# Seven products for eight: Strassen's form in a transformer layer's first MLP product

## The chip, the cores and the metric

The kernel runs on one core of one Trainium2 chip. The metric is the device time of one execution in microseconds; the figure for the kernel before is the median of three runs. Engines are called as in the profile: PE is TensorE's matmul, PEld its weight load, DVE VectorE, ACT ScalarE, POOL GpSimd, SP SyncE (here only a DMA queue).

## The reference

Two layers of a hybrid trunk over 512 latent tokens and 256 context tokens, width 1024, hidden width 4096. In each layer a modulated norm feeds one input projection, whose columns go to a gated mixer and to attention; an output projection and a gated residual follow, and then the part that matters here:

```python
x_lat = x_lat + ga2 * sqrelu_mlp(modulate(rmsnorm(x_lat, norm2_g[l]), sh2, sc2), w_ff1[l], w_ff2[l])
# the same for x_ctx in layer 0 only

def sqrelu_mlp(h, w1, w2):
    return jnp.square(jax.nn.relu(h @ w1)) @ w2
```

The shifts, scales and gates come from `silu(c) @ w_mod[l] + b_mod[l]`, six vectors of 1024 for the latents and, from `c_ctx`, for the context. In layer 1 no context output is wanted, so only its first shift and scale are needed.

## The kernel before

Activations lie feature-major: 128 features on the partitions, 768 tokens (512 latent, 256 context) along the free axis. Each float32 operand is held as two float32r tiles: `hi`, a rounded copy, and `lo`, the rest. A product of two operands is three matmuls, hi·hi, hi·lo and lo·hi, added up in PSUM. `split` makes the two parts: `act.copy` writes `hi` (L207), a subtraction on DVE writes `lo` (L208).

Weights come in blocks of 128 x 1024 float32 (512 KB) in the order that `block_order` writes down. `pump` issues the next load on SP's queue into one of two `raw` buffers and splits it into one of four `hi`/`lo` slots; `take` hands a block to a product, `release` gives its slot back, and after a delay in the program's virtual time (`fl`, a clock in ns that the matmuls advance) `settle` pumps again.

The MLP of a layer is `ff1_first` and then `steady`:

- `ff1_first` computes the first four hidden tiles (128 hidden features each, 8 k-tiles deep) while the norm's two parts, context and latents, get ready one after the other.
- A chunk `ch` of `steady` is four hidden tiles. It runs one `ff1` tile of the next chunk, the second product's share of this chunk (`proj4`: 8 output tiles of 4 k-tiles, `gate` L790 adds each from PSUM into the residual `X`, scaled), and three more `ff1` tiles. Layer 0's tokens go in two parts of 384 (`DENSE`), so a hidden tile is 8 x 3 x 2 = 48 matmuls.
- `relu2` turns a hidden tile in PSUM into squared relu, again as `hi` and `lo`: ACT relu (L960), ACT square (L965), DVE square and subtraction (L966, L967).

Beside layer 0's MLP run layer 1's modulation vectors (`mod_wide`): for each of 12 columns of 512, eight loads of 256 KB; per load and condition ACT multiplies by the input (L374), POOL adds (L375); then DVE transposes and reduces (L386, L387) and four tiny matmuls finish (L392). `more()` emits the next step of that generator. `consts` prepares a layer's constants (rotary factors `G`, norm gains, the mixer's weights): two loads on ACT's queue, one on SP's, small DVE operations (L566 to L579).

The order in which each engine issues is made by a list scheduler when the program is built. Inside `manual_schedule(engines=...)` the named engines keep the order in which the code emits; the others are reordered. For layer 0's MLP, `PAR["FM0"]` is `'DA'`: DVE and ACT keep the emitted order in chunks 0 to 6.

## Time and profile before

| what | value |
|---|---|
| median of three runs | 1515.79 us (1515.77 to 1517.52) |
| the profiled execution: its time | 1516.59 us |
| its span, first to last instruction | 1514.8 us |
| granted TensorE clock, mean | 0.995 |
| instructions | 22788, of these 8804 matmuls |
| DMA | 148.83 MB, mean 98 GB/s |

Layer 0's MLP lies at about 380 to 915 us of the span, layer 1's begins near 1200. How to read the lines that follow: in the page's part 2 each digit is the busy share, in tenths, of one fortieth of the span (37.9 us). A row of a group is line, engine, operation, `out<-in`, shape, count, then busy us, mean ns of one instruction, and the engine's idle time just before these with the one that ended it. Matmuls are pipelined, so the mean of one is longer than the distance between two; rates are taken from a count in a stretch of time.

### The profile page before, as it was taken

Reading aid. Unit: us, or ns where it says so; the run is one execution under the profiler, and the core shown is the slowest. Engines: PE = TensorE matmul, PEld = TensorE weight load, DVE = VectorE, ACT = ScalarE, POOL = GpSimd, SP = SyncE. Lnnn points to the kernel's source line nnn. Section 1 sums busy time; section 2 is a strip of 40 time slices with the busy share of each in tenths; the row PEclk is TensorE's granted clock in tenths of the full one; section 3 lists DMA queues with packets and bytes.
Section 4 is the critical chain, followed back from the end, with each engine's and each line's share of the span. In section 5 each row is a group of like instructions: output and inputs, shape, how many; then the busy total and the mean of one; then the engine's idle time right before and its main releaser. Section 6 shows DMA issues by size and latency. Waiting matters only on the chain.

```text
span 1514.8 us, 22788 instructions
## 1 busy us (share of the span) xinstructions
PE 1463.9 (97%) x8804; PEld 1316.3 (87%) x8804; DVE 959.7 (63%) x1874; ACT 682.4 (45%) x1142; POOL 403.5 (27%) x362
## 2 busy tenths in 40 slices
PE   6999899999999999999999999998999999999998
PEld 2899687787899999999999988996899888888887
DVE  5877967787755455555555548888887644444443
ACT  3542455674445454544545334535784333322221
POOL 0112421312054555554545513044212000000000
PEclk9999999999999999999999999999999999999999
DMA  9221344401234333343434311321001323333332
GB/s 362 66 71 55 118 177 156 138 1 42 74 105 132 112 112 125 112 125 98 134 103 127 107 45 56 98 70 56 29 1 56 112 98 98 98 97 97 96 95 76
DMA packets 49948, 148.83 MB, mean 98 GB/s; under 512 B 5424, under 2 KB 6832, under 8 KB 49840
## 3 DMA queue, kind: packets, MB, share of 16 engines
q1 hardware_dynamic: 49264, 146.46, 30.2%
q8 instruction: 69, 1.13, 0.3%
q10 hardware_dynamic: 576, 0.92, 0.2%
q14 instruction: 39, 0.32, 0.1%
HBM read 145.26 MB, written 2.10 MB: 97 GB/s over the span
## 4 chain that ended last, share of the span: by engine, by line
PE 79%; DVE 12%; ACT 3%; DMA 3%; issue 1%; POOL 0%; SPq 0%; ACTq 0%; DVEq 0%; POOLq 0%
PE pa L203 51%; PE pb L203 20%; PE pt L203 3%; PE pt L850 3%; DVE lo L208 1%; PE pb L332 1%; ACT hi L207 1%; DMA raw<-in_w_tok 1%; DMA B<-in_w_mod 1%; DMA A<-in_w_mod 1%; DVE m L283 1%; DVE B L967 1%; DVE m L831 1%; ACT w L834 1%; DVE A L853 1%
## 5 line engine op out<-in xcount | busy, mean ns | idle before, releaser
L203 PE MATMUL pa<-A,hi 128*128 128x384 f32 (+2 forms) x1696 | 449.1, 347 | 1.9 <-ACT w L960 0.6
L207 ACT CAST hi<-raw 128x1024 fp32r<-128x1024 f32 x171 | 179.5, 1050 | 408.9 <-PE pa L203 325.9
L208 DVE TENSOR_TENSOR lo<-raw,hi 128x1024 fp32r<-128x1024 f32 x155 | 203.3, 1312 | 216.5 <-ACT hi L207 213.1
L203 PEld LDWEIGHTS pa<-A,hi 128*128 128x128 f32 x1696 | 304.7, 188 | 26.0 <-ACT w L960 1.8
L375 POOL TENSOR_TENSOR C<-C,s 128x512 f32<-128x512 f32 x168 | 240.4, 1462 | 244.7 <-ACT s L374 244.7
L203 PE MATMUL pa<-A,lo 128*128 128x384 f32 (+2 forms) x848 | 293.6, 347 | 1.1 <-DVE lo L208 1.1
L203 PE MATMUL pa<-B,hi 128*128 128x384 f32 (+1 forms) x900 | 246.5, 356 | 4.4 <-DVE X L790 4.4
L203 PEld LDWEIGHTS pa<-B,hi 128*128 128x128 f32 x900 | 162.9, 188 | 21.6 <-DVE X L790 9.4
L790 DVE SCALAR_TENSOR_TENSOR X<-pa,modT,X 128x384 f32<-128x384 f32 (+1 forms) x168 | 88.0, 547 | 141.9 <-PE pa L203 141.7
L203 PEld LDWEIGHTS pa<-A,lo 128*128 128x128 f32 x848 | 159.3, 188 | 12.3 <-DVE lo L208 1.5
L203 PE MATMUL pa<-B,lo 128*128 128x384 f32 (+1 forms) x450 | 158.1, 353 | 0.0
L203 PE MATMUL pb<-B,hi 128*128 128x256 f32 (+2 forms) x600 | 152.8, 341 | 0.4 <-DVE X L790 0.4
L374 ACT ACTIVATE s<-k,silu 128x512 f32<-128x512 f32 x168 | 114.3, 716 | 47.1 <-DMA k<-in_w_mod 27.6
L203 PE MATMUL pb<-hi,A 128*128 128x256 f32 x672 | 126.2, 285 | 0.0
L203 PEld LDWEIGHTS pb<-B,hi 128*128 128x128 f32 x600 | 103.9, 189 | 11.4 <-DVE X L790 1.0
L790 DVE SCALAR_TENSOR_TENSOR X<-pb,modT,X 128x512 f32<-128x512 f32 (+3 forms) x116 | 69.0, 602 | 69.0 <-PE pb L203 68.8
L203 PEld LDWEIGHTS pb<-hi,A 128*128 128x128 f32 x672 | 106.1, 191 | 0.2 <-issue 0.2
L203 PE MATMUL pb<-B,lo 128*128 128x256 f32 (+2 forms) x300 | 101.6, 339 | 0.0
L203 PE MATMUL pb<-lo,A 128*128 128x256 f32 x336 | 95.3, 284 | 0.0
L203 PEld LDWEIGHTS pa<-B,lo 128*128 128x128 f32 x450 | 84.4, 188 | 5.9
L434 POOL TENSOR_TENSOR acc<-acc,s 128x256 f32<-128x256 f32 (+1 forms) x43 | 47.0, 1092 | 138.7 <-ACT s L432 138.2
L834 ACT ACTIVATE w<-pa,m 128x768 f32<-128x768 f32 (+1 forms) x80 | 65.7, 821 | 38.2 <-DVE m L831 29.8
(171 smaller groups left out, 2321.9 us busy)
## 6 DMA issues: line engine op xcount, KB each, us to landing
raw<-in_w_ff SPq DMA_DIRECT2D x128, 512.0 KB, 3.5
k<-in_w_mod SPq DMA_DIRECT2D x96, 256.0 KB, 2.9
raw<-in_w_tok SPq DMA_DIRECT2D x19, 512.0 KB, 3.6
raw<-in_w_out SPq DMA_DIRECT2D x16, 512.0 KB, 3.5
lo<-in_w_mod SPq DMA_DIRECT2D x16, 512.0 KB, 4.5
hi<-in_w_mod SPq DMA_DIRECT2D x16, 512.0 KB, 3.7
A<-in_w_mod SPq DMA_DIRECT2D x8, 512.0 KB, 10.0
raw<-in_w_u SPq DMA_DIRECT2D x8, 512.0 KB, 3.6
```

The costliest lines, as they stand in the source:

```text
L203: pe.matmul(out, a, b, start=start, stop=stop)
L207: act.copy(hi, src)
L208: (eng or vec).tensor_tensor(out=lo, in0=src, in1=hi.bitcast(F32), op=ALU.subtract)
L283: vec.tensor_scalar(yi, v.bitcast(I32), -0.5, 1595932665.0, op0=ALU.mult, op1=ALU.add)
L332: pe.matmul(ps[q:q + 32, :], S32[:, k, :], ws_[k2 // 2][:, k2 % 2 * 512:(k2 % 2 + 1) * 512], start=k < ns, stop=k >= KT - ns)
L374: act.activation(p, w, AF.Copy, scale=s)
L375: pool_e.tensor_tensor(out=a, in0=a, in1=p, op=ALU.add)
L434: eng.tensor_tensor(out=self.acc, in0=self.acc, in1=sq, op=ALU.add)
L790: vec.scalar_tensor_tensor(out=xs, in0=src[:, s - off:e - off], scalar=modT[l][:, i * 8 + m, cond:cond + 1], in1=xs, op0=ALU.mult, op1=ALU ...
L831: vec.tensor_reduce(out=nmx, in_=ps[:, 0:nk], axis=AX.X, op=ALU.max, negate=True)
L834: act.activation(p, ps[:, 0:nk], AF.Exp, bias=nmx, accum_out=sm)
L850: pe.transpose(tp_[:, (kt - k0) * 128:(kt - k0) * 128 + 128], p[:, kt * 128:kt * 128 + 128], ident)
```

## The change

In layer 0 the first product is done, for 14 pairs of hidden tiles (p, p + 16), in the form of Strassen as Winograd wrote it: weights in a 2 x 2 grid (hidden halves by input halves), tokens in a 2 x 2 grid (input halves by token halves of 384), seven block products and additions before and after instead of eight products. The other four tiles (0, 16, 1, 17) stay in `ff1_first`.

- Weights: a new `factor` loads both tiles of a pair, splits a11 and a12 (`al`), forms four differences and sums on POOL in place, then splits the sums (`be`), the differences (`ga`) and a22 (`q`, in a pair of half-wide tiles of its own).
- Tokens: `factors` forms the token sums `TT` once, from the second pass of `ff1_first` through chunk 0's second product (POOL adds hi and lo, DVE subtracts, ACT and DVE split).
- `ff1_pair` runs the seven products on four PSUM banks, with ACT copies and DVE and POOL adds between, and squares the relus.
- Hidden tiles get buffers of their own, H0 to H3, one each; in a chunk both pairs come first, then the second product, whose first three output tiles run their first half of k ahead (`early`). Its parts are 512 and 256 instead of 384 and 384 in all of layer 0's chunks.
- `FM0` is `''`: all engines are reordered in layer 0's MLP.
- `mod_wide` leaves out the context half of eight columns, yields after nearly each add instead of each load, and defers its last step by `MF`; it starts in chunk 1, not 0.
- Layer 1's `consts` move from before the steady chunks to behind chunk 7. Several small tiles move into H0 to H3, and the scratch of dynamic DMAs is set to 1024 bytes. The rows of `w_ff2` are laid out in the new order of hidden tiles.

The diff, cut to its core:

```diff
-       "FM0": 'DA', "FM1": '', ...
+       "FM0": '', "FM1": '', ...  "MF": 6000.0, ...
@@ block_order
+        if l == 0:
+            o += [("ff1", l, m) for m in (0, 16, 1, 17)]
+            for ch in range(8):
+                if ch:
+                    a, b = 2 * ch, 2 * ch + 1
+                    o += [("al", l, a), ("be", l, a), ("al", l, b), ("ga", l, a), ("be", l, b), ("ga", l, b)]
+                o += [("ff2", l, ch, nb) for nb in range(4)]
+            continue
@@ beside pump
+    def factor(key):
+        kind, l, p = key
+        hi, lo = slot()
+        if kind == "al":
+            ra = ring.tile([128, 1024], F32, tag="raw", name=nm("raw"), bufs=2)
+            nc.sync.dma_start(ra, w_ff1[l, p])
+            rb = unit(("B6", "C0")[p % 2], [128, 1536], F32)
+            nc.sync.dma_start(rb[:, 512:1536], w_ff1[l, p + 16])
+            raws[p] = ra, rb
+            split(hi, lo, ra)
+            a11, a12, s2, a21, a22 = ra[:, 0:512], ra[:, 512:1024], rb[:, 0:512], rb[:, 512:1024], rb[:, 1024:1536]
+            tt = pool_e.tensor_tensor
+            tt(out=a11, in0=a11, in1=a21, op=ALU.subtract)
+            tt(out=a21, in0=a21, in1=a22, op=ALU.add)
+            tt(out=s2, in0=a22, in1=a11, op=ALU.subtract)
+            tt(out=a12, in0=a12, in1=s2, op=ALU.subtract)
+        elif kind == "be":
+            split(hi, lo, raws[p][1][:, 0:1024])
+        else:
+            ra, rb = raws.pop(p)
+            split(hi, lo, ra)
+            qh, ql = (ring.tile([128, 512], F32R, tag=t, name=nm(t), bufs=1) for t in ("qh", "ql"))
+            split(qh, ql, rb[:, 1024:1536])
+            ready.append((("q", l, p), qh, ql))
+        ...
@@ mod_wide
+            conds = range(2 if j < 4 else 1)
+            acc = unit("C1", [128, 3, 512], F32)
...
-                if k not in PAR["YK"]:
-                    yield
+                    if k > 1 or k and cond:
+                        yield
...
+            fl.defer(PAR["MF"], fin)
@@ consts
+        kg = unit("H2", [128, 1664], F32)
+        k2 = kg[:, 0:640]
...
+        ws = unit("H3", [128, 2, 512])
@@ proj4: the first three output tiles, first half of k ahead
+                    if early and pi == 0 and m < 3:
+                        if m == 0:
+                            ...
+                            for i in range(3):
+                                for q, (off, n) in enumerate(parts):
+                                    fm_mms(ed[i][q][:, 0:n], ew[i], off, n, 0, 2)
+                                fl.tick()
+                        for q, (off, n) in enumerate(parts):
+                            fm_mms(ed[m][q][:, 0:n], ew[m], off, n, 2, 4)
+                            gate(i_, m, off, n, ed[m][q])
+                            ...
@@ layer
+        def product(dst, w, wo, rhs, first, last_):
+            for k in range(4):
+                whi, wlo = (a[:, wo + k * 128:wo + k * 128 + 128] for a in w)
+                rhi, rlo = rhs(k)
+                for i, (a, b) in enumerate(((whi, rhi), (whi, rlo), (wlo, rhi))):
+                    pe.matmul(dst, a, b, start=first and k == 0 and i == 0, stop=last_ and k == 3 and i == 2, skip_group_check=True)
+                    fl.vt += hn / 2.4 + 13.0
+            fl.tick()
+
+        def ff1_pair(p):
+            ...
+            ps = pa()
+            A, C = ps[:, 0:hn], ps[:, 512:512 + hn]
+            B, E = pb()[:, 0:hn], pt()[:, 0:hn]
+            ...
+            al = take("al", l, p)
+            product(A, al, 0, quad(0, 0), True, True)
+            act.copy(c1_, A)
+            be = take("be", l, p)
+            product(C, be, 512, tsum(0), True, True)
+            act.copy(c5, C)
+            more()
+            product(A, al, 512, quad(1, 0), False, True)
+            release()
+            r = tsm([128, hn])
+            act.activation(r, A, AF.Relu)
+            hd = H[p]
+            act.activation(hd[:, 0, 0:hn], r, AF.Square)
+            tt(out=r, in0=r, in1=r, op=ALU.mult)
+            tt(out=hd[:, 1, 0:hn], in0=r, in1=hd[:, 0, 0:hn].bitcast(F32), op=ALU.subtract)
+            more()
+            product(B, be, 0, tsum(1), True, True)
+            release()
+            tt(out=U2, in0=B, in1=c1_, op=ALU.add)
+            more()
+            product(E, take("q", l, p), 0, tsum(3), True, True)
+            ga = take("ga", l, p)
+            product(B, ga, 0, tsum(2), False, True)
+            tt(out=U3, in0=B, in1=c1_, op=ALU.add)
+            pool_e.tensor_tensor(out=c5, in0=c5, in1=U3, op=ALU.add)
+            t21 = tsm([128, hn])
+            tt(out=t21, in0=E, in1=U3, op=ALU.add)
+            put(p + 16, 0, sqrelu(t21))
+            more()
+            product(C, ga, 512, quad(1, 1), False, True)
+            release()
+            tt(out=U2, in0=C, in1=U2, op=ALU.add)
+            put(p, 1, sqrelu(U2))
+            put(p + 16, 1, sqrelu(c5))
+            more()
@@ steady
+                if strassen:
+                    if ch:
+                        ff1_pair(2 * ch)
+                        ff1_pair(2 * ch + 1)
+                    R = [H.pop(m) for m in (2 * ch, 2 * ch + 16, 2 * ch + 1, 2 * ch + 17)]
...
-                passes, post = [list(dense)], None
+                passes, post = [[(0, SEQ), (SEQ, CTX)] if strassen else list(dense)], None
...
+                if strassen:
+                    if end:
+                        K1.append(consts(l + 1))
```

`put(m, j, sq)` writes token half j of a hidden tile: ACT copies `hi`, DVE subtracts `lo`. `sqrelu` is one DVE operation.

## The prediction

> **What bounds the kernel now.** First the page: which engine has no time left.

> ```profile
> span 1514.8 us, 22788 instructions
> PE 1463.9 (97%) x8804; PEld 1316.3 (87%) x8804; DVE 959.7 (63%) x1874; ACT 682.4 (45%) x1142; POOL 403.5 (27%) x362
> PE   6999899999999999999999999998999999999998
> DVE  5877967787755455555555548888887644444443
> POOL 0112421312054555554545513044212000000000
> PEclk9999999999999999999999999999999999999999
> PE 79%; DVE 12%; ACT 3%; DMA 3%; issue 1%; POOL 0%; SPq 0%; ACTq 0%; DVEq 0%; POOLq 0%
> ```

> TensorE (PE) is busy 97% of the span at full clock, and 79% of the chain that ended last is matmuls. A busy PE need not be an efficient one, so the next view cuts layer 0's MLP, which the change rewrites, at its chunk boundaries (columns: stretch, its us, then busy us and instructions of PE, weight load, VectorE (DVE), ScalarE (ACT), GpSimd (POOL), clock, DMA share, GB/s).

> ```profile
> 383.00:408.00 25.00, 24.34 (x113) 19.72 (x113) 20.60 (x31) 13.04 (x22) 3.51 (x2) 1.00 0.17 53
> 408.00:554.20 146.20, 145.27 (x847) 142.55 (x846) 81.43 (x111) 72.21 (x97) 74.10 (x52) 1.00 0.39 120
> 623.00:692.00 69.00, 68.16 (x402) 66.81 (x402) 35.99 (x50) 32.93 (x45) 33.34 (x25) 1.00 0.36 111
> 833.90:895.00 61.10, 61.10 (x352) 58.16 (x351) 31.51 (x49) 22.32 (x29) 19.33 (x14) 1.00 0.31 92
> ```

> One steady chunk (four hidden tiles of the first product, then a quarter-depth part of the second) takes 69.0 us; DVE is busy 52% of it, ACT and POOL 48%. Next, the rate inside a chunk, from pieces of the chain of waits (start, us, what, count), and all of PE's waits from 383 to 895 us (total, times, longest):

> ```profile
> 572.75 2.08 PE pa L203 x12
> 939.32 5.46 PE pb L203 x24
> 982.38 5.81 PE pb L203 x48
> ```

> ```profile
> PE pa L203 <- DVE X L790: 4.4, 5, 1.3
> PE pa L203 <- ACT w L960: 0.6, 1, 0.6
> ```

> Twelve 384-wide matmuls take 2.08 us: 173.3 ns each. The other pieces, from layer 1, are 512 wide (227.5 ns) and 256 wide (121.0 ns). A steady chunk has 4 x 48 + 192 = 384 matmuls of 384, which is 66.6 us; 2.4 us of 69.0 are small modulation matmuls and stalls, and PE's own waits come to only 5.0 us in 512. This stage is matmuls end to end: what is taken from PE comes off the time, until another engine cannot keep up.

> **The change part by part.** *Matmuls.* For two hidden tiles p and p+16 the old form issues 2 x 8 x 3 x 2 = 96 matmuls of 384, the new one 7 products x 4 x 3 = 84. Tiles 0, 16, 1, 17 keep the old form, so 14 pairs change: 168 x 173.3 ns = **-29.1 us**. The second product's 512+256 costs 348.5 ns where 384+384 costs 346.7: 7 chunks x 96 x 1.8 ns = **+1.2 us** (chunk 7 has these parts already). A chunk is then 29.1 + 33.5 = 62.6 us of matmuls.

> *What pays for it: DVE, ACT, POOL.* The rows from 410 to 890 us (busy us, mean ns, idle before), and POOL's adds over the run (min/median/max ns):

> ```profile
> L208 DVE TENSOR_TENSOR lo<-raw,hi 128x1024 fp32r<-128x1024 f32 x57 | 82.8, 1453 | 107.7 <-ACT hi L207 107.7
> L967 DVE TENSOR_TENSOR B<-w,B 128x768 fp32r<-128x768 f32 x24 | 36.6, 1527 | 0.8
> L966 DVE TENSOR_TENSOR w<-w 128x768 f32<-128x768 f32 x27 | 25.8, 957 | 9.9 <-ACT B L965 8.9 <-ACT C L965 0.7
> L790 DVE SCALAR_TENSOR_TENSOR X<-pa,modT,X 128x384 f32<-128x384 f32 x42 | 25.7, 613 | 13.1 <-PE pa L203 12.9
> L386 DVE STREAM_TRANSPOSE s<-C 128x512 f32<-128x512 f32 x24 | 16.8, 702 | 0.0
> L387 DVE TENSOR_REDUCE m<-s 128x16 f32<-128x512 f32 x24 | 16.5, 686 | 0.8
> L569 DVE TENSOR_TENSOR G<-w,k 128x128 f32<-128x128 f32 x4 | 1.1, 282 | 0.0
> L208 DVE TENSOR_TENSOR ws<-raw,ws 128x512 fp32r<-128x512 f32 x1 | 0.7, 693 | 0.8 <-ACT ws L207 0.8
> ```

> ```profile
> L374 ACT ACTIVATE s<-k,silu 128x512 f32<-128x512 f32 x166 | 112.9, 716 | 45.7 <-DMA k<-in_w_mod 27.6 <-POOL C L375 17.9
> L207 ACT CAST hi<-raw 128x1024 fp32r<-128x1024 f32 x57 | 59.8, 1048 | 149.9 <-PE pa L203 135.7 <-PE pt L203 14.2
> L960 ACT ACTIVATE w<-pa 128x512 f32<-128x512 f32 x2 | 1.2, 590 | 0.0
> ```

> ```profile
> L375 POOL TENSOR_TENSOR C<-C,s x168: 1274/1296/2292, 393.9 to 860.6; 128x512 f32<-128x512 f32 x168
> ```

> DVE, per pair: weight splits 3 x 1.45 + 0.69 = 5.0 us (before 2.9); four adds out of PSUM x 0.61 = 2.4 and eight 384-wide SBUF operations, half a 768-wide row each (0.48 to 0.76, taken as 0.7), 5.6, against 2 x (0.96 + 1.53) = 5.0 before. That is +5.1 us a pair, 71 us in 14. The gates lose their third instruction, and eight modulation columns lose their context half (8 x 1.39 = 11 us). A chunk has about 43 us of DVE, 69% of 62.6. ACT: casts 3 x 1.05 + 0.62 and seven 384-wide operations of about 0.5 per pair, four casts for the second product (4.2 us) and some 17 modulation multiplies x 0.716 per chunk (18 steps of one each, less those that transpose): 31 us, 49%. POOL: four weight sums x 1.46 and one 384-wide add near 1.1 per pair, 17 modulation adds x 1.46: 39 us, 62%. None is full, so I price this work at nothing beside PE and pay for the places where its latency can show:

> - *Inside a pair* two matmul groups accumulate on a bank that another engine must read first: product 3 behind ACT's copy of A, product 6 behind DVE's first U2 add. The cover of each is one product, 2.08 us. The add takes 0.61, so it may come 1.4 us late; a DVE instruction that has just started takes up to 1.5, rarely more. Bounds per pair: nothing, to 1.0 us (blocked splits at both places). I take 0.3, nearer the low end, as most of DVE's instructions are far shorter than 1.4: **+4.2 us**.
> - *Chunk ends.* No next tile stands between the pairs and the second product now; its first three output tiles run on the first pair's hidden tiles instead, 3 x 6 x 348.5 ns = 6.3 us of cover. The last tiles need the U2 add, two squared relus, two copies and two low parts: 4 to 5 us of DVE, 6 to 7.5 with a split in between. Before, a chunk paid up to 2.4 us here. Bounds for the difference: -2 to +3 a chunk; I take **0**.
> - *First chunk.* The fifth hidden tile, which ran from 408.5 to 417.7 us (first the tile's own first matmul, then the second product's), goes. The relu chain of the last two first tiles, which ended only at 416, has the second product directly behind it:

> ```profile
> 408.54 0.51 PE L203 MATMUL pa<-A,hi 128*128 128x384 f32 x2
> 417.69 0.51 PE L203 MATMUL pa<-B,hi 128*128 128x384 f32 x2
> ```

> ```profile
> 410.76 0.69 DVE L966 TENSOR_TENSOR w<-w 128x512 f32<-128x512 f32 x1
> 415.28 0.69 DVE L967 TENSOR_TENSOR B<-w,B 128x512 fp32r<-128x512 f32 x1
> ```

> Half-depth parts of three output tiles in free order cover 6.3 us. The token sums (8 POOL adds of 768 at 1.5 x 1.296 = 1.9 us, 16 DVE subtractions and 16 low parts x 0.55) queue on a DVE that is 82% busy from 383 to 408, partly ahead of those relus. Bounds 0 to 5; I take **+1.0**.
> - *Weights.* The loads move the same bytes: SP's queue issues two together where it issued one. ACT and DVE casts of one slot wait for PE's release as before; the chain of POOL sums (5.8 us alone, about 10 with modulation between) starts when the first split has read the raw weights, some 17 us ahead of the product that uses its result, for the second pair too. Cost 0; if that cover is gone, 1 to 3 us a pair.
> - *Layer 1's constants* move from the start of the MLP behind its last matmul, since they now lie in H2 and H3. Two loads on ACT's queue wait for PE's last read of H2, ahead of the norm's squares; one load on SP's queue, eight G operations x 0.28, a split of 0.69 and an ACT cast go in front of the layer boundary, where DVE is eight tenths busy. Layer 1's first key product (96 matmuls x 121 ns = 11.6 us) covers them. Bounds 0 to 5; **+1.0**.
> - *Free order* of DVE and ACT adds no instruction. With the later, evenly spread modulation it is in the bounds above; so are the new buffers.

> Sum: -29.1 + 1.2 + 4.2 + 0 + 1.0 + 1.0 = **-21.7 us** against this execution's 1516.59 us (span 1514.8 and 1.8 around it), 0.8 above the median of 1515.79; so **1494 us**. With the low ends (no pair stall, chunks 1 to 2 us better, 0 for the rest) it is 1474 to 1481, with the high ends 14 + 21 + 5 + 5 it is slower by 17.

> **A rule beside the rows.** L208 takes 1453 ns on average beside POOL's adds. Its durations (min/median/max) in layer 1's MLP, where POOL does next to nothing, and in this stage:

> ```profile
> L208 DVE TENSOR_TENSOR lo<-raw,hi x52: 1224/1226/1226, 1212.3 to 1489.7; 128x1024 fp32r<-128x1024 f32 x52
> L208 DVE TENSOR_TENSOR lo<-raw,hi x57: 1212/1226/2190, 409.6 to 882.2; 128x1024 fp32r<-128x1024 f32 x57
> ```

> So beside POOL some take 1 us more, and POOL's adds go from 1.27 to 2.29: they look like two engines taking turns. [...] By the rule at its worst, each of a chunk's ten full splits blocked as long as the longest here (2.19 us), DVE has 7 us more per chunk than at the mean of 1.453, 50 of 62.6, and the sum stays as it is; the rule can move the time only through waits, which the first rival prices.

> **Rivals.** *Taking turns becomes the bound (slower).* Undisturbed durations of what takes turns, per chunk: DVE 10 splits x 1.226, two of 0.69, sixteen 384-wide x 0.55 = 22.5 us; POOL 25 x 1.296 + 2.1 = 34.5; together 57 us of 62.6 (91%), where the old chunk had 17.5 + 32.4 = 50 of 69 (72%). If two independent queues fill that resource to 85% only, a chunk takes 67 us; the forecast's 21.7 over 7 chunks are gone at 62.6 + 3.1 = 65.7, that is below 87%. At 80% a chunk takes 71.3: 1494 + 7 x 8.7 = 1555. For it: the 2.2 us durations. Against it: the adds out of PSUM, on which PE waits, have one SBUF input, POOL's modulation is not urgent, and PE waited 5.0 us only at 72%.

> *Every pair waits.* A late copy or add costs 1 us a pair instead of 0.3: 1494 + 10 = 1504; 1.5 us: 1511. For it: DVE stood 107.7 us behind ACT's casts, blocking what was behind. Against it: it did so mostly with nothing else to do.

> *The cover holds better than I think:* pair and chunk stalls vanish, 1478 to 1484.

> *The change does not do what it says:* the removed matmuls come back as waits of the same size, 1513 to 1519, as above with 1.8 us a pair.

> **How the numbers follow.** Forecast (1484 to 1505) 0.62; each pair waits longer (1505 to 1512.8) 0.15; cover better (below 1484) 0.05; given back (within 0.2%, some 3 us, about what a measurement can tell from no change) 0.06; slower 0.12. Faster 0.82, same 0.06, slower 0.12. The range 1483 to 1512 leaves out the last two and the ends.

> **What would show it.** Right: 84 matmuls a pair at 173 ns, steady chunks near 65 us, PE's waits on DVE and ACT in this stage below 15 us in all, the 512-wide part 1.8 ns dearer or not at all. Wrong: PE waiting for the U2 add or the copy of A over 1 us a pair (second rival); DVE's 384-wide and POOL's 512-wide durations near 1.5 and 2.3 us and chunks over 66 us (first); a gap behind 408 us over 2 us (first chunk); DVE's G operations in the chain at the boundary (constants).

## The result and the profile after

The changed kernel takes **1592.7 us** (1590.9 to 1593.8, four runs) where the kernel before takes 1516.65 (1515.8 to 1520.3, four runs): a ratio of **1.0492**, 95% interval 1.0479 to 1.0504. It is 76 us slower; I had forecast 1494 us.

The page of the changed kernel:

```profile
span 1591.6 us, 22495 instructions
PE 1472.3 (93%) x8636; PEld 1282.3 (81%) x8636; DVE 1030.7 (65%) x1974; ACT 669.7 (42%) x1164; POOL 429.2 (27%) x384
PE   6999899989787979898989899998999999999999
PEclk9999999999899988899999999999999999999999
PE 60%; DVE 21%; ACT 6%; POOL 5%; DMA 4%; issue 4%; SPq 0%; POOLq 0%; DVEq 0%; ACTq 0%
```

The matmuls did go: 8636 in place of 8804, 168 fewer, as counted. But in slices 10 to 24, layer 0's MLP, PE's digits go between 7 or 8 and 9 where they stood at 9, and the granted clock falls in some of them. The last row is the clearest: of the chain that ended last, matmuls fell from 79% to 60%, VectorE rose from 12% to 21%, ScalarE from 3% to 6%, GpSimd from 0% to 5%. PE no longer sets the pace there. One chunk (778.9 to 854.1, columns as in the forecast's windows) and the largest of PE's waits in layer 0's MLP:

```profile
778.90:854.10 75.20, 67.34 (x378) 60.62 (x377) 44.72 (x60) 33.57 (x50) 40.40 (x30) 0.95 0.42 140
```

```profile
PE pa L211 <- DVE X L844: 33.3, 13, 5.4
PE pa L1122 <- ACT w L1142: 14.5, 6, 4.4
PE pa L211 <- DVE H L1111: 11.0, 7, 2.7
PE pa L211 <- ACT w L1038: 6.2, 3, 4.3
PE pb L211 <- DVE lo L216: 3.0, 1, 3.0
PE pa L211 <- DVE w L1171: 2.9, 2, 1.6
```

This chunk takes 75.2 us instead of 69.0 (it is the shortest; they go up to 83.4), and none of the other engines is full in it: DVE 59%, POOL 54%, ACT 45%. Yet PE waits 71 us where it waited 5.0: for the gates that empty PSUM (L844), for ACT's copy of A in the second pair of a chunk (L1142), for the pairs' last hidden parts (L1111, L1171), and in the first chunk (L1038, L216). What a gate was late for is seen in the chain of waits, here in the middle of the second product (start, us, what):

```profile
675.62 0.73 ACT C L424
...
678.08 1.29 POOL C L425
679.37 1.26 POOL raw L294
...
680.70 1.29 POOL B L295
682.00 1.26 POOL B L296
683.25 1.25 POOL C L425
...
684.53 0.02 ACT C L424
...
685.16 1.03 ACT hi L215
...
686.29 1.76 DVE lo L216
688.05 0.67 DVE X L844
...
688.77 2.93 PE pa L211 x12
```

Read it from the end. PE stands still until 688.77 because a gate, a 0.67 us operation whose input was ready since about 684.2, ran only at 688.05. On DVE's queue it stood behind a weight split's low part (L216), which needs ACT's cast (L215); on ACT's queue that cast stood behind a modulation multiply (L424), whose product buffer a GpSimd addition (L425) still had to read; and that addition stood on GpSimd's queue behind the weight sums (L294 to L296). DVE stood idle for 3.47 us ahead of that low part, the last 2 of them with the gate ready behind it. Work that is not urgent, on three queues that wait for each other in a ring, holds up urgent work by order alone. The rows around it show the second loss:

```profile
684.50:687.82 3.32, 1.00 (x5) 0.49 (x3) 1.53 (x1) 1.66 (x2) 2.47 (x2) 1.00 0.00 0
687.83:694.66 6.83, 5.89 (x22) 5.41 (x23) 2.12 (x4) 0.00 (x0) 0.00 (x0) 0.50 0.24 77
694.70:702.40 7.70, 7.70 (x44) 6.68 (x44) 2.95 (x4) 1.05 (x1) 4.27 (x4) 1.00 0.00 0
```

Behind PE's idle stretch the clock is granted at 0.50 for 6.83 us: PE is back, but its 22 matmuls take 5.9 us, in which some 40 would run at full clock. In all stretches at 0.50 of this trace a matmul of 256, 384 or 512 columns starts 213, 320 or 427 ns ahead of the next (medians), where it is 120, 173 or 227 at full clock.

The account of layer 0's MLP, from the distances between the starts of neighbouring matmuls (columns/2.4 + 14 ns is fitted to the 120, 173 and 227 ns at full clock; what exceeds it is a gap): matmuls -29.1 + 1.2, as forecast; gaps 91.2 us against 15.5, **+75.7**; matmuls at half clock, in 12 stretches of 3.4 or 6.8 us, 68 us in all, **+25.2**. Together +73.0 of the 76.8 us between the two spans. From the first matmul of layer 1's product to the end it is 589.7 us before and 592.9 after: **+3.3** more, which the part on the prediction traces to layer 1's constants. That leaves 0.5 us open.

### The profile page after: what moved, and what is told of

The parts are those of the page before. It is cut to its first block, busy times and chain, and to the rows that moved or that the text cites. A ratio compares the mean times of both kernels' runs of the same rounds, so it can differ in the third digit from the quotient of the medians.

```text
span 1591.6 us, 22495 instructions
## 1 busy us (share of the span) xinstructions
PE 1472.3 (93%) x8636; PEld 1282.3 (81%) x8636; DVE 1030.7 (65%) x1974; ACT 669.7 (42%) x1164; POOL 429.2 (27%) x384
## 3 DMA queue, kind: packets, MB, share of 16 engines
q8 instruction: 68, 1.11, 0.3%
## 4 chain that ended last, share of the span: by engine, by line
PE 60%; DVE 21%; ACT 6%; POOL 5%; DMA 4%; issue 4%; SPq 0%; POOLq 0%; DVEq 0%; ACTq 0%
PE pa L211 29%; PE pb L211 18%; PE pa L1122 5%; DVE lo L216 3%; PE pt L928 2%; DMA k<-in_w_mod 2%; POOL C L425 2%; ACT hi L215 2%; PE pb L1122 1%; PE pt L211 1%; DVE w L1114 1%; DVE m L909 1%; DVE A L931 1%; PE pb L379 1%; ACT w L912 1%
## 5 line engine op out<-in xcount | busy, mean ns | idle before, releaser
L215 ACT CAST hi<-raw 128x1024 fp32r<-128x1024 f32 x171 | 179.4, 1050 | 396.1 <-PE pa L211 252.7
L216 DVE TENSOR_TENSOR lo<-raw,hi 128x1024 fp32r<-128x1024 f32 x155 | 195.3, 1260 | 120.7 <-ACT hi L215 117.2
L211 PE MATMUL pa<-A,hi 128*128 128x512 f32 (+2 forms) x800 | 223.2, 365 | 8.7 <-ACT w L1038 6.2
L211 PE MATMUL pa<-H,hi 128*128 128x256 f32 (+1 forms) x688 | 185.0, 359 | 47.7 <-DVE X L844 33.3
L211 PEld LDWEIGHTS pa<-H,hi 128*128 128x128 f32 x688 | 126.2, 203 | 73.5 <-DVE X L844 39.7
L844 DVE SCALAR_TENSOR_TENSOR X<-pa,modT,X 128x512 f32<-128x512 f32 (+1 forms) x128 | 84.5, 661 | 138.3 <-PE pa L211 138.2
L211 PEld LDWEIGHTS pa<-A,hi 128*128 128x128 f32 x800 | 144.5, 190 | 33.6 <-ACT w L1038 8.0
L425 POOL TENSOR_TENSOR C<-C 128x512 f32<-128x512 f32 x84 | 121.8, 1450 | 104.8 <-ACT C L424 103.6
L211 PE MATMUL pa<-A,lo 128*128 128x512 f32 (+2 forms) x400 | 144.2, 362 | 1.1 <-DVE lo L216 1.1
L1122 PE MATMUL pa<-A,hi 128*128 128x384 f32 x448 | 119.9, 349 | 14.5 <-ACT w L1142 14.5
L211 PE MATMUL pa<-H,lo 128*128 128x512 f32 (+1 forms) x344 | 118.6, 353 | 0.0
L844 DVE SCALAR_TENSOR_TENSOR X<-pb,modT,X 128x512 f32<-128x512 f32 (+3 forms) x114 | 69.5, 616 | 74.5 <-PE pb L211 74.2
L211 PE MATMUL pb<-B,hi 128*128 128x512 f32 (+1 forms) x404 | 101.7, 342 | 0.0
L424 ACT ACTIVATE C<-k,silu 128x512 f32<-128x512 f32 x84 | 60.0, 720 | 78.0 <-POOL C L425 39.2
L211 PE MATMUL pa<-B,hi 128*128 128x512 f32 x300 | 92.4, 389 | 0.0
L211 PEld LDWEIGHTS pa<-A,lo 128*128 128x128 f32 x400 | 75.9, 190 | 12.2 <-DVE lo L216 1.3
```

What stands on the lines that cost most here:

```text
L211: pe.matmul(out, a, b, start=start, stop=stop)
L215: act.copy(hi, src)
L216: (eng or vec).tensor_tensor(out=lo, in0=src, in1=hi.bitcast(F32), op=ALU.subtract)
L424: act.activation(p, w, AF.Copy, scale=s)
L425: pool_e.tensor_tensor(out=a, in0=a, in1=p, op=ALU.add)
L844: vec.scalar_tensor_tensor(out=xs, in0=src[:, s - off:e - off], scalar=modT[l][:, i * 8 + m, cond:cond + 1], in1=xs, op0=ALU.mult, op1=ALU ...
```

## The experiments

Where no other count is given a time is one execution; the kernel before took 1516.8 to 1519.1 us beside them. Thirteen executions of the kernel before in the last batch lie between 1515.1 and 1521.0 us, so two single times less than about 5 us apart show no difference.

**The parts of the change, one at a time.** *fixed_order* is the changed kernel with the old order of DVE and ACT; *old_free* is the kernel before with the free order alone:

```diff
-       "FM0": '',        # fixed_order: in the changed kernel
+       "FM0": 'DA',
-       "FM0": 'DA',      # old_free: in the kernel before
+       "FM0": '',
```

> The changed kernel with FM0 back at 'DA': VectorE and ScalarE keep the emitted order in chunks 0 to 6 of layer 0's MLP, all else as changed. Theory 'order' (the built order of the free queues puts instructions that wait for GpSimd ahead of gates and copies that PE needs): 1500 to 1535, the gate waits in the middle of the second product (35.7 us) gone for the most part. Rival 'GpSimd is too slow' (the chain of weight sums and modulation adds is late whatever the order): 1575 to 1610, waits of the same size. Rival 'no order helps, emitted order is worse': over 1610.

> The kernel before with FM0 at '' alone. Theory 'free order by itself costs': over 1540, with PE gaps of 3 us as after the change. Rival 'free order is harmless without the weight sums and the tighter chunk': 1510 to 1525.

fixed_order 1573.4 us, old_free 1572.9. The free order by itself, one string in an otherwise unchanged program, costs the old kernel **56 us**; and the new kernel is 57 us too slow in the old order too. So no single part carries the loss. old_free came out as its first theory said. fixed_order fell just below the range of 'GpSimd is too slow': the gate waits did go, from 33.3 to 4.3 us, but those for the copy of A grew from 14.5 to 20.1, other waits came up, and half clock still cost some 17 us (25 before). The page's part 4, the largest of PE's waits in layer 0's MLP and a piece of the chain of waits, of old_free:

```profile
PE 67%; DVE 13%; ACT 6%; DMA 5%; POOL 5%; issue 4%; SPq 0%; ACTq 0%; POOLq 0%; DVEq 0%
PE pa L203 41%; PE pb L203 19%; POOL C L375 4%; DMA k<-in_w_mod 3%; PE pt L850 2%; ACT s L374 2%; PE pt L203 2%; DVE lo L208 1%; ACT hi L207 1%; DMA X<-in_xT 1%; PE pb L332 1%; DMA C<-in_w_mod 1%; DMA A<-in_w_mod 1%; DVE m L283 1%; DVE A L467 1%
```

```profile
PE pa L203 <- ACT w L960: 16.8, 5, 5.7
PE pa L203 <- DVE X L790: 16.5, 11, 3.8
```

```profile
591.24 1.28 POOL C L375
...
593.16 1.03 ACT hi L207
594.19 0.71 ACT w L960
594.95 7.29 PE pa L203 x24
```

GpSimd's modulation additions (L375), absent from the chain before, are now its third entry, and in the piece PE waits for a relu (L960) that stands on ACT's queue behind a cast (L207) and behind a multiply that waited for the addition: waits of the same kind, without any of Strassen's form.

**Which work makes the ring.** *no_sums* leaves the four weight sums of a pair out, *no_mod* multiplies and adds the modulation's first k-tile only, *no_add* keeps all of ACT's multiplies and leaves out GpSimd's additions behind them (these three compute other values than the reference), *more_buf* gives the products one buffer more:

```diff
-            tt(out=a11, in0=a11, in1=a21, op=ALU.subtract)           # no_sums
...
-                        else:                                        # no_mod
+                        elif k > 8:
-                            pool_e.tensor_tensor(out=a, in0=a, in1=p, op=ALU.add)   # no_add
+                            two = [acc[:, 2, :]] + [acc[:, 1, :]] * (j > 3)         # more_buf
+                            i = nprod % (len(two) + 1)
+                            p = tsm([128, 512]) if j < 4 and cond else two[i] if i < len(two) else tmp.tile([128, 512], F32, tag="acc0", name=nm("acc0"), bufs=1)
```

> The changed kernel without the four GpSimd weight sums of a pair; the splits take the raw weights instead, so the hidden values are not the reference's. Theory 'GpSimd chain in the way' (a split waits for sums, and gates stand behind the split): 1525 to 1550, the 35.7 us of gate waits down to under 12. Theory 'order': 1560 to 1590, as other instructions take the blocking place. The copy of A waiting behind the first pair's last copies (15.8 us) should stay in both.

> The changed kernel without 84% of the modulation's multiplies and adds (only the first k-tile of each column is used; loads, transposes and sums stay), so layer 1's modulation is not the reference's. Theory 'GpSimd chain in the way': 1510 to 1540, since the sums then run without adds in between and nothing takes turns with VectorE half of the time. Theory 'order': 1560 to 1590. If modulation does not matter at all: 1590.

> The changed kernel without GpSimd's modulation adds; ScalarE's multiplies and all loads stay, so layer 1's modulation is not the reference's. Theory 'GpSimd' (its adds make ScalarE wait and take turns with VectorE): about 1510, as without the multiplies. Rival 'ScalarE' (its multiplies wait for their loads, and copies and casts stand behind them): 1560 or more. Between, 1525 to 1550, both take part.

> The changed kernel with one more buffer for the products that GpSimd adds (two instead of one, three instead of two). Theory 'ScalarE waits for GpSimd's buffer' (39 us of its idle time): 1550 to 1575. Rival 'the wait moves elsewhere': 1580 to 1600.

no_sums 1558.1, no_mod 1508.1, no_add **1512.9**, more_buf 1580.9. Leaving out the weight sums gives back 35 us of the loss, GpSimd's 112 modulation additions 80; the two overlap, as their sum is more than the loss. Without the additions, with every multiply still on ACT, the kernel takes 4 us less than the one before, which however still has its own additions; the old form without any was not run. Another order is not the reason: of the instructions that both have, 1966 of 1974 on DVE, 1161 of 1164 on ACT and all 272 on POOL start in the same sequence in no_add as in the changed kernel, while the free order of old_free moved 188 of 1874 on DVE and 204 of 1142 on ACT. One more buffer gives 12: a little slack does not open the ring. no_add and, at the edge of its range, more_buf's rival came out as written; no_mod fell 2 us below its range, and no_sums between its two, though the gate waits did come down to 11.1 us and the copy of A still cost 14.5. Two chunks of no_add, and DVE's SBUF operations there:

```profile
587.00:651.20 64.20, 64.13 (x369) 58.21 (x368) 36.90 (x58) 28.99 (x44) 12.52 (x11) 1.00 0.31 103
717.60:783.20 65.60, 64.84 (x378) 58.45 (x378) 38.77 (x60) 33.42 (x50) 12.30 (x11) 1.00 0.49 161
```

```profile
L1113 DVE SCALAR_TENSOR_TENSOR w<-w 128x384 f32<-128x384 f32 x28 | 15.5, 553 | 6.6 <-POOL w L1163 6.6
L1110 DVE TENSOR_TENSOR H<-w,H 128x384 fp32r<-128x384 f32 x28 | 15.2, 550 | 1.3 <-ACT H L1109 1.1
```

These are the chunks near 65 us that I had forecast. The matmuls' saving is real, and pairs, chunk ends and weights cost next to nothing once GpSimd is mostly idle: PE's waits there are 6.0 us for gates and 0.7 for the copy of A; 9 us more remain in the first chunk.

**Turns at SBUF, or waits in queues?** An addition on GpSimd does two things: ACT waits for it, and beside it DVE's operations with both inputs in SBUF last longer. In the changed kernel's layer 0 MLP, of its sums, differences and squares of this kind on 384, 512 or 1024 columns none of the 174 that started while GpSimd was not adding is over 8 ns above its undisturbed time (0.55, 0.69 or 1.22 us); of the 54 that started during a modulation addition 47 are 0.13 to 1.11 us above it. The additions themselves go from 1.30 us (median) to 2.25 at most. That is what taking turns means below. *write_only* keeps the waits and the time, but what replaces the additions reads nothing: three memsets of the product buffer in place of each modulation addition.

```diff
-                            pool_e.tensor_tensor(out=a, in0=a, in1=p, op=ALU.add)
+                            for _ in range(3):
+                                pool_e.memset(p, 1.0)
```

> The changed kernel with each of GpSimd's modulation adds replaced by three fills of the product's buffer: the same waits on ScalarE and by ScalarE, about the same GpSimd time, but nothing read from SBUF; layer 1's modulation is not the reference's. Theory 'taking turns' (VectorE and GpSimd block each other when both read): 1515 to 1535, VectorE's long durations gone beside modulation. Rival 'late chain' (ScalarE waits for a busy GpSimd, casts and copies stand behind it): 1570 to 1595.

1543.2 us, between the two ranges: both take part. In this view of the operations concerned the first two rows are the changed kernel's, the others write_only's:

```profile
L1114 DVE SCALAR_TENSOR_TENSOR w<-w 128x384 f32<-128x384 f32 x28 | 27.2, 972 | 7.1 <-POOL w L1164 7.1
L1111 DVE TENSOR_TENSOR H<-w,H 128x384 fp32r<-128x384 f32 x28 | 22.6, 814 | 0.2
```

```profile
L1115 DVE SCALAR_TENSOR_TENSOR w<-w 128x384 f32<-128x384 f32 x28 | 15.3, 552 | 4.7 <-POOL w L1165 4.7
L1112 DVE TENSOR_TENSOR H<-w,H 128x384 fp32r<-128x384 f32 x28 | 15.0, 551 | 0.3
L426 POOL MEMSET C<- 128x512 f32 x252 | 130.1, 527 | 87.5 <-ACT C L424 76.9 <-issue 4.2
```

Three memsets last 1.58 us, a little more than an addition (1.45 beside DVE's work), and GpSimd is as busy as before, but DVE's operations are back at their undisturbed 0.55 us (553 and 550 ns in no_add): 0.55 us beside memsets, which only write, 0.81 and 0.97 on average beside additions, which read as well. So of the 80 us that the additions cost, taking turns makes some **49** and GpSimd's time as such some **30**. These 30 are ACT's waiting for GpSimd together with the weight sums that stand behind the fills on GpSimd's queue; no run parts the two. The split is rough: each side is one execution, and 19 instructions on DVE and 17 on ACT stand in another place than in the changed kernel.

**Modulation on VectorE.** The parameter `MP` moves both multiply and add of the modulation to one DVE operation. It was tried in both kernels and in both orders:

```diff
-       "MP": [0, 1],
+       "MP": [],         # dve_mod, dve_fixed (with FM0 'DA'); old_dve, old_free_dve in the kernel before
```

> The changed kernel with MP = []: the modulation is one multiply-add on VectorE per step, 116 of about 0.69 us and 20 plain multiplies, none on ScalarE or GpSimd. Theory 'chain over three queues' (ScalarE behind GpSimd behind VectorE): 1500 to 1535 although VectorE gets 11 us more per chunk. Rival 'VectorE's load': over 1575.

> The kernel with the modulation on VectorE and FM0 = 'DA'. Theory 'order' alone: 1510 to 1520. Rival (the emitted order keeps the first pair's last copies ahead of the second pair's copy of A, 2 us per chunk): 1530 to 1545.

> The kernel before with the modulation on VectorE (MP = []), order as before. If GpSimd's adds cost the old kernel its 2 us of stalls per chunk: 1503 to 1512. If not: 1515 to 1520; over 1525 if VectorE then holds the gates back.

> The kernel before with FM0 = '' and the modulation on VectorE. It separates the product's form from the rest: against the changed kernel with the modulation on VectorE (1526.8). If GpSimd's adds under a free order are the cause in both kernels: 1510 to 1525, that is 48 to 63 below the 1573 of free order alone. If free order is costly by itself: over 1550.

| layer 0's MLP | old order, additions on POOL | free order, on POOL | old order, on DVE | free order, on DVE |
|---|---|---|---|---|
| kernel before | 1515.8 | 1572.9 | 1563.2 | 1518.2 |
| changed kernel | 1573.4 | 1592.7 | 1565.5 | 1526.8 |

The table is the answer to which part was wrong: none of the three by itself. The emitted order suits the old form with additions on POOL, the free order suits modulation on DVE, and the other two columns are 47 to 77 us above the old time in either kernel. The changed kernel is slower by 9 to 58 us in three columns; the 2 us of the third are within the spread. Its row holds all other parts of the change too (fewer context columns, constants later), which no run takes apart. dve_mod and old_free_dve came out as their theories said and old_dve as its last case; dve_fixed missed both of its ranges by 20 us or more. In old_dve PE waits 29.7 us for gates, in old_free_dve 3.7: the chain of the former has multiply-adds (L379, 0.75 us each) right in front of gates, again order on one queue. Why the scheduler's order is the better one here and the worse one with additions on POOL stays open: the durations that it assumed do not show in a trace.

**What is left with modulation on DVE.** dve_mod's chunks take 66.6 to 69.3 us, still above 65. *dve_tok* puts the token sums' eight additions on DVE as well, *late_tokens* (in the changed kernel) and *tok_shift* (in dve_tok) make the token sums later, *act_some* and *act_all* (in dve_tok) move squares from DVE to ACT. The edits, cut to their core:

```diff
-                    pool_e.tensor_tensor(out=v, in0=h2[kk][:, 0, 0:TQ]..., op=ALU.add)     # dve_tok
+                    vec.tensor_tensor(out=v, in0=h2[kk][:, 0, 0:TQ]..., op=ALU.add)
-        sums = [factors(), False]                                                          # late_tokens
+        sums = [factors(), True]
-                    if strassen and ch == 0 and n % 2:
+                    if strassen and ch == 0:
-                    if pi and n_ >= 6 and n_ % 2 == 0 and strassen and not sums[1]:        # tok_shift
+                    if pi and n_ >= 16 and strassen and not sums[1]:
-            put(p + 16, 0, sqrelu(t21))                                                    # act_some
+            act.activation(t21, t21, AF.Relu)
+            act.activation(t21, t21, AF.Square)
-            vec.scalar_tensor_tensor(out=t, in0=t, scalar=0.0, in1=t, op0=ALU.max, op1=ALU.mult)   # act_all
+            act.activation(t, t, AF.Relu)
+            act.activation(t, t, AF.Square)
```

> The kernel with the modulation on VectorE (MP = []) and also the eight additions of the token sums on VectorE instead of GpSimd. If the loss at the first chunk is GpSimd's 2 us adds and their turns: 1513 to 1520, the gaps at 402 to 427 us down to under 3 us. If it is VectorE's load: 1527 or more.

> The changed kernel with the token sums begun in chunk 0, none of them in the second pass of the first four tiles. Theory 'token sums block the relus' (gaps of 4.5, 3.2 and 1.7 us at 402 to 427 and half clock in two stretches of 6.8 us): 1576 to 1584, 8 to 16 less. Rival 'the sums are then late for chunk 1': 1590 or more, with the gap in front of the first pair.

> The 1522.5 kernel with the token sums emitted from step 16 of the second pass on, one at each step, instead of from step 6 at every second. If the sums stand in front of the relus at the start: 1515 to 1520, the gaps at 410 to 421 us (5.9 us) down to 2. If they are only moved under the first chunk's gates: 1521 to 1525.

> As the kernel with all squares on ScalarE, but only the first two squares of a pair (two VectorE operations less); the last two, which the second product waits for, stay. Theory 'VectorE's load': 1512 to 1518. If the chain at the chunk's end matters more than the load, this one is faster than the one with all four.

> The 1522.5 kernel (modulation and token additions on VectorE) with the squares of the hidden values on ScalarE (relu, square, copy), four VectorE operations of 0.55 us less per pair. Theory 'VectorE's load is what is left' (chunks of 67 us where the matmuls need 62.6): 1505 to 1514. Rival 'the longer chain of ScalarE operations is late at the chunk's end': 1525 or more.

dve_tok 1522.5, late_tokens 1585.4, tok_shift 1523.9, act_some 1526.4, act_all 1530.5. dve_tok fell between its two ranges. Taking all squares from DVE to ACT costs 8 us, and taking half of them does not help, as act_all's rival said and act_some's theory did not, so DVE's load alone is not the residue; that a square on ACT is one more handover between queues is argued, not shown. Moving the token sums moves PE's gaps (tok_shift has one of 6.6 us at 420, late_tokens five between 416 and 460) and does not make them fewer: from 388 to 470 us dve_tok has 12.2 us of them, tok_shift 13.0; the changed kernel 14.5, late_tokens 17.2. tok_shift's second case held; late_tokens is 7 us faster than the changed kernel, 1 above the range of its theory, but not by shorter gaps in this stretch.

**Room for the token sums.** *classic1* is dve_tok with chunk 1 in the old form (12 pairs left) and the token sums spread over chunks 0 and 1. In it part of chunk 1's tokens are replaced by their sums before its tiles read them, so it computes other values than the reference; *classic2* makes these last four sums only after chunk 1's fourth tile. Both also emit the modulation's steps at other places (`more`), so the token sums are not the only thing that differs from dve_tok.

```diff
+                if ch == 1:
+                    o += [("ff1", l, m) for m in (2, 18, 3, 19)]
...
+                    if ch == 1:
+                        for m in (2, 18, 3, 19):
+                            ff1(m)
+                            for _ in range(4 if m == 19 else 3):
+                                next(sums[0], None)
+                        more(2)                                          # classic2, cut to its core
```

> The 1522.5 kernel (modulation and token additions on VectorE) with chunk 1's four tiles in the old form too (12 pairs left) and the token sums spread from chunk 0 to chunk 1's tiles, none in the first pass. 24 more matmuls of 384 cost 4.2 us. Theory 'the first chunk loses some 13 us to token sums in front of relus and gates': 1510 to 1516. Rival 'the loss moves to chunk 1': 1522 to 1530.

> The version with modulation and token sums' additions on VectorE, with chunk 1 put back in the old form (12 pairs of Strassen's form are left, 24.9 us fewer matmuls by the forecast's price) and the token sums spread over chunks 0 and 1, the last of them only after chunk 1's tiles have read the tokens that they overwrite. If the first chunk's token sums are what is left of the loss: 1506 to 1511 us, and no idle stretch of TensorE above 3 us between 390 and 460 us. If the residue comes from the pairs themselves: above 1515 us, since two pairs of the saving (4.2 us) are given up and nothing is gained.

classic1, four executions, 1507.9 us, ratio 0.9939 (0.9921 to 0.9957); classic2, eight executions, **1514.4** (1510.7 to 1516.2) against 1517.5, ratio **0.9973** (0.9960 to 0.9985). PE's waits from 388 to 462 us, first dve_tok's two largest, then all of classic2's:

```profile
PE pa L211 <- DVE X L844: 4.0, 2, 3.1
PE pa L211 <- ACT w L1038: 2.0, 1, 2.0
```

```profile
PE pa L213 <- DVE A L522: 0.5, 1, 0.5
PE pa L213 <- ACT w L1040: 0.4, 1, 0.4
```

The first chunk's stalls are gone, as expected, and giving up two pairs (4.2 us) makes the kernel 8 us faster than dve_tok (6.5 with each held against the kernel before in its own batch). The times were missed: classic1 is 2 us below its range, classic2 3.4 us above its 1506 to 1511. One of classic2's chunks takes 71.4 us where classic1's takes 67.8; why was not tried. So a version with Strassen's form beats the kernel before, by 0.15% to 0.40% and not by the 1.4% that I forecast. The largest part of the rest of its saving stands here, as PE's waits for the gates in layer 0's MLP:

```profile
PE pa L213 <- DVE X L846: 12.8, 15, 2.1
```

with DVE busy 54.4 of the 66.1 us of a late chunk. The same account as above, each trace to the end of this MLP: 144 matmuls fewer -24.9, wider parts about +1, gaps 31.6 against 15.5 (+16.1), half clock +1.4, behind the MLP +3.6: -2.8, where the profiled spans differ by -1.5.

## Why the prediction was wrong, point by point

- *Matmuls, -29.1, and 512 + 256, +1.2*: right. 168 of 384 columns and 96 + 96 of the second product in each chunk, at unchanged distances (173 and 227 + 120 ns). no_add has chunks of 64.2 and 65.6 us.
- **"None is full, so I price this work at nothing"**: this step failed. It took an engine's share of busy time for its price. The work itself came out as forecast (DVE 44.7, POOL 40.4 and ACT 33.6 us in the chunk above, where I had 43, 39 and 31); what cost 80 us was GpSimd's additions beside DVE, whose 384-wide operations went from 0.55 to 0.81 and 0.97 us, and three queues that wait for each other in a ring, with PE's gates behind both. I had quoted the ring's rows (DVE 107.7 us idle behind ACT's casts, ACT 17.9 us behind POOL's additions) and dismissed the first as idleness with nothing else to do.
- **"Free order ... adds no instruction ... it is in the bounds above"**: failed in the same way. That the order costs no instruction says nothing: old_free is the old program in another order, and 56 us slower. I gave it neither a term nor a rival.
- *Inside a pair, 0.3 us (0 to 1.0)*: the place was named rightly, product 3 behind ACT's copy of A, but not the reason: 14.5 us in 6 waits, 1.0 a pair, the upper bound. One of them in the chain of waits:

```profile
638.58 1.02 POOL w L1164
...
641.16 0.56 DVE s L1114
...
641.74 0.92 ACT H L1110 x2
642.66 0.39 ACT w L1142
...
643.09 3.91 PE pa L1122 x12
```

  The copy itself takes 0.48 us on average; it stands on ACT's queue behind the casts that end the pair before (L1110), these wait for DVE's square (L1114), and that stood behind one that waits for GpSimd's c5 addition (L1164). In no_add the wait is 0.7 us in all.
- *Chunk ends, 0 (-2 to +3)*: the last hidden parts cost 11.0 + 2.9 us over seven chunks, 2.0 each, inside the bounds, at the dear end: DVE's operations there took 0.81 and 0.97 us where I had 0.7.
- *First chunk, +1.0 (0 to 5)*: PE waits 13 us there (4.1 + 5.7 + 3.0 + 0.5), and matmuls at half clock add some 6. I had named the queueing ("partly ahead of those relus") and priced the cover against DVE alone; POOL's eight additions took 2.57 us each in place of 1.9 (one took 4.8), and ACT's relu stood behind ACT's casts of the sums.
- *Weights, 0 ("if that cover is gone, 1 to 3 us a pair")*: the cover did go, at the gates: no_sums is 35 us faster, 2.5 a pair, and has 11.1 us of gate waits for 33.3. That this lies in the alternative's range is partly luck: I looked for the product that needs the sums and not for what queues behind them, and the 35 us hold the sums' share of the turns at SBUF too, which is small: in the changed kernel's trace one DVE operation of those counted above started beside a weight sum (L216 at 523.1, 2.30 us in place of 1.22).
- *Layer 1's constants, +1.0 (0 to 5)*: too small inside its bounds, **3.3 us**, and not by the DVE operations that I named. From the first matmul of layer 1's product to the end it is 589.7 us in the kernel before, 589.5 in old_free and 589.4 in old_free_dve; the changed kernel takes 592.9, and its six variants fixed_order, no_add, dve_mod, dve_tok, classic1 and classic2 take 593.0 to 594.9. In the changed kernel the constants' load (`wsT`) takes one of the two `raw` buffers at 996.56, so layer 1's second weight block (`w_u`), issued 2 us ahead of that product in the kernel before, is issued 11 us behind its start, and its low part comes late. In the chain of waits:

```profile
1009.26 0.46 ACT H L215
1009.72 4.11 DMA raw<-in_w_u
...
1013.86 1.06 ACT hi L215
...
1020.34 5.73 PE pa L211 x24
```

- *Taking turns becomes the bound (slower)*, the rival that ended on this side: right in sign, and its rows were the right ones: DVE's 384-wide operations near 1 us, chunks over 66. By its own measure 57 us of undisturbed work in chunks of 78 us on average (75.2 to 83.4) is 73%, where I had priced 85 and 80%. One thing that I held against it did hold: the adds out of PSUM (L1158, L1163, L1166, L1171) took 540 to 559 ns, also the eight that started during an addition on GpSimd, and no gate took over 753 ns, where 67 started during one (on 512 columns the median in layer 1's MLP, with GpSimd idle, is 751); they were late, not long. write_only shows why the loss overshot: turns explain some 49 us, and waiting in queues, which was no rival of mine, some 30. Chance 0.12 was too low for a resource forecast at 91%.
- *Every pair waits* and *the change does not do what it says* priced PE's waits by pairs up to 1.8 us; measured are 71 us, 5 a pair, most of it outside the pairs.
- *A clock that drops behind idle time* was in no term: **25 us**, a third of the loss, which comes along with gaps of some 3 us and more.

## What to carry to other kernels

Price moved or added work by what stands behind it on its engine's queue, not by its engine's busy share (here a 0.67 us gate ran 3.9 us after its input was ready, behind a split whose input was late, though DVE was idle for 2 of them): follow each urgent operation (here the gates and the copy that opens PE's next group) back through its queue to the slowest non-urgent one, above all where a multiply, an addition and a split pass between three engines. A scheduler's order is a change of its own: the same instructions cost 56 us more in another order, and which order is good depended on the engine that did the non-urgent work. And where what takes turns is forecast at 91% of a stage, as here, take it for the bound first and not for a rival: here the stage came out at 73%.
